# Rounded weight parts from a second transfer on GpSimd's queue, and SSD products in halves of 64 columns, in a hybrid SSD/HGRN2 encoder layer

## The chip, the cores and the metric

The kernel runs on one core of a Trainium2 chip. The metric is the device time of one execution in microseconds (us); the time of a kernel is the median of several executions. TensorE is called PE in the profile (PEld is its loading of stationary operands), VectorE DVE, ScalarE ACT, GpSimd POOL, SyncE SP. A transfer is issued by an engine's queue (SP's or POOL's here) and carried out by 16 DMA engines that all queues share.

## The reference

One encoder layer on 512 tokens of width 1024. Everything is float32.

```
mod = silu(c) @ ada_w + ada_b           # shift1, scale1, gate1, shift2, scale2, gate2
h = rmsnorm(x) * (1 + scale1) + shift1
proj = h @ w_in                         # z, xbc, dt, q, f_fwd, f_bwd, i, g
y_ssd = ssd_mixer(z, xbc, dt, ...)      # 16 heads x 64, state 128, both directions
y_hg  = hgrn2_mixer(q, f_fwd, f_bwd, i, g, ...)   # 8 heads, 128 x 128, both directions
x = x + gate1 * (concat(y_ssd, y_hg) @ w_out)
h = rmsnorm(x) * (1 + scale2) + shift2
x = x + gate2 * (relu(h @ w_up)**2 @ w_down)      # d_ff = 4096
return rmsnorm(x)
# inside the SSD scan, per chunk and head:
w = scores * decay * dt
y_intra = einsum("btsgh,bsghp->btghp", w, xc)
```

## The kernel before

**Two-part products.** To reach float32 accuracy with TensorE's fp32r type, each operand of a weight product is held as two fp32r parts: `hi`, the value rounded to fp32r, and `lo`, the remainder. A product is three matmuls, hi x hi, hi x lo and lo x hi, accumulated in PSUM. The products inside the recurrences are plain float32 matmuls.

**Weights.** Weights come in units: 256 output columns by 1024 rows, in four quarters of 256 rows, each quarter a tile of 128 partitions x 2 x 256 (256 KB). `unit_load` issues the transfers of a unit's quarters from SP into tiles `raw` (four buffers). `unit_split` calls `split` for the quarters asked for: it takes a tile `hi` and a tile `lo` (seven buffers each), lets ScalarE copy `raw` to `hi`, which rounds, and VectorE compute `lo = raw - hi`. `wl_load` does the same for the last column quarter of w_out into tiles `wohi` and `wolo` (eight buffers).

**Units ahead.** While the products of one unit run, the next is loaded, and its quarters 1 to 3 are split at the unit's start; the fourth is split by `last()`, from a hook in the unit's last pass. So the fourth quarter of the next unit gets the buffer of the current unit's first quarter, the seventh before it.

**Stages**, in us of the profiled span: startup with norms and modulation (0 to 68; its own copies of weights, 16 quarters in `su_split`, are not touched by the change); the units of w_in other than z, mixed with the steps of the SSD and HGRN2 recurrences (68 to 459); the four z units (459 to 522); w_out's first 512 columns in 16 iterations, three ahead (522 to 571); its third column quarter in four groups of 4 x 128 rows (574 to 597); its last column quarter from `wohi`, `wolo` (597 to 625); the MLP as four blocks of four up units and four dn units (625 to 989). In the background, rows of `ada_w` are loaded (`adaw`, 512 KB each, from POOL's queue) and summed by VectorE into the later modulation rows (`ada`).

**Order.** TensorE keeps the order in which the code is written. `Clock` adds up estimated costs of what was emitted for TensorE, VectorE and ScalarE; `tick()`, called between products, advances the recurrences' step generators when the clock says they are due and the two vector engines are less than 3.5 us ahead of TensorE. The order on the other engines is set by the framework's scheduler when the program is built. A queue runs in order: an instruction or transfer that waits holds all that stand behind it on its engine.

**SSD.** For each group of heads and each of four blocks of 128 tokens, `load` fetches the cumulated decays of four heads (tile `e`, and `bc` for the other direction, read from the scratch tensor `cdr`) over POOL's queue; `decay` turns them into `es`, 128 x 4 x 128; `intra` multiplies them with `xs`, 64 columns a head, into `ps_y`. `V`, `K`, `Q`, `S`, `kt`, `at`, `hy` and `T` are tiles of the HGRN2 steps.

**Product loops.** `mm_T` has the weights as the stationary side (w_in's transposed units, up), `mm_N` as the moving side; both take a unit's quarters in order, three matmuls for each 128 rows.

Of the kernel before, what the change touches and what calls it, by code (L numbers as in the profile page):

```python
# [9 lines left out]
F32 = mybir.dt.float32  # L10
F32R = mybir.dt.float32r
# [3 lines left out]
MULT, ADD, SUB, MIN, MAX = ALU.mult, ALU.add, ALU.subtract, ALU.min, ALU.max  # L15
PSUM = bass.MemoryType.PSUM

P = 128
# [35 lines left out]
class Clock:  # L54
# [3 lines left out]
    def __init__(self):  # L58
        self.pe = self.dve = self.act = 0.0
        self.done = {}  # L60
        self.end = 0.0
        self.table = None
# [89 lines left out]
def encoder_layer(  # L152
# [7 lines left out]
    nc = tc.nc  # L160
    clock = Clock()
    V, A, G = Timed(nc.vector, clock, "dve"), Timed(nc.scalar, clock, "act"), nc.gpsimd
# [17 lines left out]
    w_out2 = w_out.rearrange("o k n -> (o k) n")  # L180
# [6 lines left out]
    wp = ctx.enter_context(tc.tile_pool(name="wp", bufs=7))  # L187
# [10 lines left out]
    def nm(s):  # L198
        cnt[0] += 1
        return f"{s}_{cnt[0]}"  # L200

    def psum(tag):
        bufs = {"mm": 2, "sc": 3, "tr": 2, "y": 1}[tag]
        return ps.tile([P, 512], F32, tag=tag, name=nm("ps_" + tag), bufs=bufs)

    def tmp():
        return tp.tile([P, 520], F32, tag="t", name=nm("t"))
# [106 lines left out]
    h_hi = actp.tile([P, KD, T], F32R, tag="A_hi", name="h_hi")  # L314
    h_lo = actp.tile([P, KD, T], F32R, tag="A_lo", name="h_lo")

    def load_w(src, k0, nk, col0, ncols):
        raw = wp.tile([P, 544], F32, tag="raw", name=nm("raw"), bufs=4)
        v = raw[:, :nk * ncols].rearrange("p (k n) -> p k n", n=ncols)
        nc.sync.dma_start(out=v, in_=src[k0 * P:(k0 + nk) * P, col0:col0 + ncols].rearrange("(k p) n -> p k n", p=P))  # L320
        return v


    amod = const([P, 16], "amod")
# [275 lines left out]
        yield  # L600


    def split(raw, nk, ncols, lo_eng=None):
        n = nk * ncols
        hi = wp.tile([P, 544], F32R, tag="hi", name=nm("hi"))[:, :n].rearrange("p (k n) -> p k n", n=ncols)
        lo = wp.tile([P, 544], F32R, tag="lo", name=nm("lo"))[:, :n].rearrange("p (k n) -> p k n", n=ncols)
        A.copy(out=hi, in_=raw)
        (lo_eng or V).tensor_tensor(out=lo, in0=raw, in1=hi.bitcast(F32), op=SUB)
        return hi, lo

    def unit_load(src, cols, k0=0):

        ncols = sum(n for _, n in cols)
        quarters = []
        for q in range(4):
            raw = wp.tile([P, 544], F32, tag="raw", name=nm("raw"), bufs=4)
            v = raw[:, :2 * ncols].rearrange("p (k n) -> p k n", n=ncols)
            o = 0
            for c0_, n in cols:
                r = (k0 + 2 * q) * P  # L620
                nc.sync.dma_start(out=v[:, :, o:o + n], in_=src[r:r + 2 * P, c0_:c0_ + n].rearrange("(k p) n -> p k n", p=P))
                o += n
            quarters.append(v)
        return quarters, ncols

    def unit_split(u, qs=range(4)):
        quarters, ncols = u
        return [split(quarters[q], 2, ncols) for q in qs]

    def mm_T(w, j, rh, rl, nk=8, pst=None, n0=0, n=T, hook=None, ks=None):  # L630

# [98 lines left out]
    def ssd_group(g, after):  # L730
# [35 lines left out]
        es, ld = {}, {}  # L766
# [9 lines left out]
        def decay(cc, q):  # L776

            e, bc = ld[cc, q, 0], ld[cc, q, 1]
            h0 = g * 8 + 4 * q
            for d, dst in ((0, e), (1, bc)):  # L780
                if d < DEC:
                    V.tensor_tensor(out=dst, in0=dst, in1=b3(off[:, d, cc, h0:h0 + 4], 4, P), op=ADD)
                else:
                    for h in range(4):
                        A.activation(dst[:, h, :], dst[:, h, :], AF.Identity, bias=off[:, d, cc, h0 + h:h0 + h + 1])
            V.copy_predicated(out=e, mask=masks[:, NL64 * 64:].unsqueeze(1).broadcast_to([P, 4, P]), data=bc)
            A.activation(e, e, AF.Exp)
            V.tensor_tensor(out=e, in0=e, in1=cb[:, g, cc, :].unsqueeze(1).broadcast_to([P, 4, P]), op=MULT)
            es[cc, q] = e
            if q == 0:  # L790
                load(cc, 1, 0)
                load(cc, 1, 1)
            elif cc + 1 < NT:
                load(cc + 1, 0, 1)
# [4 lines left out]
        for cc in range(NT):  # L799
            yv = xs[:, cc, g * 512:(g + 1) * 512]  # L800

            def intra(q):
                for h in range(4):
                    c0_ = (4 * q + h) * 64
                    PE.matmul(out=py[:, c0_:c0_ + 64], lhsT=es[cc, q][:, h, :], rhs=yv[:, c0_:c0_ + 64], start=True, stop=True)

            decay(cc, 0)
            yield -9.0
            decay(cc, 1)
            yield  # L810
            py = psum("y")
            intra(0)
            intra(1)
            dirs = [d for d in range(2) if (d, cc) in st]
            pis = {}
            for d in dirs:
                pis[d] = psum("sc")
                PE.matmul(out=pis[d], lhsT=ct[:, g, cc * P:(cc + 1) * P], rhs=st[d, cc], start=True, stop=True)
            V.tensor_tensor(out=h3(yv), in0=h3(yv), in1=b3(coef[:, cc, hs], 8, 64), op=MULT)
            V.tensor_tensor(out=yv, in0=yv, in1=py, op=ADD)  # L820
            for d in dirs:
                ti = tmp()[:, :512]
                V.tensor_tensor(out=h3(ti), in0=h3(pis[d]), in1=b3(epre[:, d, cc, hs], 8, 64), op=MULT)
                V.tensor_tensor(out=yv, in0=yv, in1=ti, op=ADD)
            yield
            if cc + 1 < NT:
                load(cc + 1, 0, 0)
            yield
# [293 lines left out]
    cols = {"z": O_Z, "x": O_X, "q": O_Q, "ff": O_FF, "fb": O_FB, "i": O_I, "g": O_G}  # L1122
# [69 lines left out]
    korder = list(range(8, 14)) + list(range(8)) + [14, 15]  # L1192

    def mh(k, tt):
        return m_hi[k // 8][:, k % 8, tt * P:(tt + 1) * P]

    def ml(k, tt):
        return m_lo[k // 8][:, k % 8, tt * P:(tt + 1) * P]
# [5 lines left out]


    accs = [psum(t) for t in ("mm", "mm", "y", "sc")]
    wt = [split(load_w(w_out2, korder[i], 1, 0, 512), 1, 512) for i in range(3)]
    late = Stream(clock)
    late.add(mixl, xs, slack=1.0)
    x1 = None  # L1210
    for i in range(16):
        if i + 3 < 16:
            wt.append(split(load_w(w_out2, korder[i + 3], 1, 0, 512), 1, 512))
        hi, lo = wt[i]
        k = korder[i]
        for tt in range(NT):
            mm3(accs[tt], mh(k, tt), ml(k, tt), hi[:, 0, :], lo[:, 0, :], i == 0, i == 15)
            ada_on[0] = i < 12 or not ada_idle[0]
            tick()
        if late.due():  # L1220
            late.advance()
        if i == 12:
            late.drain()
            x1 = ypool.tile([P, NT, D], F32, tag="xs", name="x1")
            for tt in range(NT):
                nc.gpsimd.dma_start(out=x1[:, tt, :], in_=x2d[tt * P:(tt + 1) * P, :])
# [20 lines left out]
    wl_ = []  # L1247

    def wl_load(i):
        raw = load_w(w_out2, korder[i], 2, 768, 256)  # L1250
        hi = wo.tile([P, 2, 256], F32R, tag="hi", name=nm("wohi"))
        lo = wo.tile([P, 2, 256], F32R, tag="lo", name=nm("wolo"))
        A.copy(out=hi, in_=raw)
        V.tensor_tensor(out=lo, in0=raw, in1=hi.bitcast(F32), op=SUB)
        wl_.append((hi, lo))

    for i in range(0, 16, 4):
        ks = korder[i:i + 4]
        wq = [split(load_w(w_out2, ks[2 * q], 2, 512, 256), 2, 256) for q in range(2)]
        for tt in range(2):  # L1260
            for kk in range(4):
                k = ks[kk]
                mm3(accs1[tt][:, :256], mh(k, tt), ml(k, tt), wq[kk // 2][0][:, kk % 2, :], wq[kk // 2][1][:, kk % 2, :], i + kk == 0, i + kk == 15)
            tick()
        if i == 0:
            for tt in range(NT):
                gated_add(accs[tt], tt, 1, slice(0, 512), gate)
            accs1 += [psum("mm"), psum("mm")]
        wl_load(i)
        wl_load(i + 2)  # L1270
        for tt in range(2, NT):
            for kk in range(4):
                k = ks[kk]
                mm3(accs1[tt][:, :256], mh(k, tt), ml(k, tt), wq[kk // 2][0][:, kk % 2, :], wq[kk // 2][1][:, kk % 2, :], i + kk == 0, i + kk == 15)
            tick()
# [42 lines left out]
    for tt in range(NT):  # L1318
        o = psum(("sc", "y", "mm", "mm")[tt])
        for i in range(16):  # L1320
            k = korder[i]
            hi, lo = wl_[i // 2]
# [53 lines left out]
    for i, u in enumerate(units):  # L1376
# [13 lines left out]
        else:  # L1390
# [8 lines left out]
            if u == units[-1]:  # L1399
# [6 lines left out]
                for tt in range(NT):  # L1406
                    o = psum("mm")
# [3 lines left out]
                    r = rs2[:, tt:tt + 1]  # L1411
                    n = 448 if tt == 3 else 768
# [19 lines left out]
            for pair in range(2 if u[2] else 0):  # L1432
                o = psum("mm")
# [40 lines left out]
```

## Time and profile before

| | |
|---|---|
| median of 3 executions | 996.17 us (996.04 to 996.61) |
| the profiled execution | 997.37 us, its span 995.6 us |
| granted TensorE clock, mean | 0.992 |
| DMA traffic | 116.7 MB; SP's queue 86.45 MB, POOL's 28.32 MB |
| POOL's transfers | 32 `e`, 32 `adaw`, some few others |

The span is the time from the first to the last recorded instruction; the execution's time is 1.8 us longer. The profile names an instruction by line, engine, operation and `output<-inputs`, with buffer numbers left out; most rows have the line of a helper that records every instruction (L106 for vector operations, L170 for matmuls). A group's row has its busy time, the mean length of one in ns, and after the second bar the time for which the engine stood idle just before such instructions, with what ended most of that.

### The profile page before, as it was taken

The page shows a single profiled execution, that of the slowest core. Times are in us where ns is not written, and L with a number is a line of the kernel's source. Part 1 is how long each engine was busy: PE and PEld are TensorE (multiplying, and loading weights), DVE is VectorE, ACT ScalarE, POOL GpSimd, SP SyncE. Part 2 cuts the span into 40 slices and gives each one's busy share as a digit, 9 for nine tenths or more (in the row PEclk, how much of TensorE's full clock was granted, in tenths as well). Part 3 has the DMA queues.
Part 4 walks back from the last instruction along what each step waited for, and adds up shares of the span by engine and source line. Part 5 has one row for each costly group of instructions (what it writes and reads, how often), then busy time and mean ns, then how long its engine had stood idle before and what let it go on. Part 6 is the DMA issues. An engine that isn't in the chain of part 4 may idle for free.

```text
span 995.6 us, 17588 instructions
## 1 busy us (share of the span) xinstructions
PE 962.5 (97%) x6886; PEld 843.9 (85%) x6886; DVE 649.2 (65%) x1189; ACT 493.9 (50%) x965; POOL 48.1 (5%) x91
## 2 busy tenths in 40 slices
PE   5999999999999999989999999999999999999997
PEld 4788887788877888879998899979988998998897
DVE  4478869887989475877777677665544455444445
ACT  6367647857675366565555225642233234214414
POOL 0000000010000000000111211000000000000000
PEclk9999999999999989999999999999999999999999
DMA  9953422334422333222656875133332233223322
GB/s 272 266 134 82 111 76 64 86 96 127 109 81 77 97 106 84 66 75 65 191 168 191 283 244 147 58 114 100 98 114 85 86 105 106 88 85 96 105 66 85
DMA packets 114791, 116.70 MB, mean 117 GB/s; under 512 B 8556, under 2 KB 103445, under 8 KB 114709
## 3 DMA queue, kind: packets, MB, share of 16 engines
q1 hardware_dynamic: 106213, 86.45, 29.7%
q0 software_dynamic: 8064, 28.32, 9.2%
q8 instruction: 54, 0.88, 0.4%
q10 hardware_dynamic: 432, 0.82, 0.2%
q14 instruction: 28, 0.23, 0.1%
HBM read 113.39 MB, written 2.16 MB: 116 GB/s over the span
## 4 chain that ended last, share of the span: by engine, by line
PE 87%; DVE 4%; DMA 3%; ACT 3%; issue 2%; SPq 0%; DVEq 0%; ACTq 0%; POOLq 0%
PE ps_mm L170 65%; PE ps_sc L170 13%; PE ps_tr L170 4%; PE ps_y L170 3%; PE ps_tr L175 2%; DMA raw<-in_w_in_dram 1%; DMA e<-cdr 1%; DVE K L106 1%; ACT hi L106 1%; DMA adaw<-in_ada_w_dram 1%; ACT t L106 1%; DVE lo L106 0%; DVE ada L106 0%; DVE Q L106 0%; DVE t L106 0%
## 5 line engine op out<-in xcount | busy, mean ns | idle before, releaser
L106 ACT CAST hi<-raw 128x512 fp32r<-128x512 f32 (+1 forms) x276 | 167.1, 614 | 240.7 <-PE ps_mm L170 156.7
L106 DVE TENSOR_TENSOR lo<-raw,hi 128x512 fp32r<-128x512 f32 (+1 forms) x276 | 185.5, 681 | 108.4 <-ACT hi L106 106.2
L170 PE MATMUL ps_mm<-hi,uh 128*128 128x256 f32 x448 | 125.8, 281 | 0.0
L170 PE MATMUL ps_mm<-hi,ul 128*128 128x256 f32 x448 | 125.4, 280 | 0.0
L170 PE MATMUL ps_mm<-lo,uh 128*128 128x256 f32 x448 | 125.4, 280 | 0.0
L170 PE MATMUL ps_mm<-hi,h_hi 128*128 128x256 f32 (+1 forms) x384 | 114.3, 298 | 0.0
L170 PE MATMUL ps_mm<-h_hi,hi 128*128 128x512 f32 x256 | 107.9, 422 | 1.1 <-ACT h_hi L106 1.1
L170 PE MATMUL ps_mm<-lo,h_hi 128*128 128x256 f32 (+1 forms) x384 | 108.2, 282 | 0.0
L170 PE MATMUL ps_mm<-hi,h_lo 128*128 128x256 f32 (+1 forms) x384 | 108.1, 282 | 0.0
L170 PE MATMUL ps_mm<-h_hi,lo 128*128 128x512 f32 x256 | 101.7, 397 | 0.0
L170 PE MATMUL ps_mm<-h_lo,hi 128*128 128x512 f32 x256 | 101.5, 397 | 0.0
L170 PE MATMUL ps_mm<-m_hi,hi 128*128 128x512 f32 (+1 forms) x264 | 100.7, 381 | 0.7 <-ACT m_hi L106 0.7
L170 PE MATMUL ps_mm<-m_lo,hi 128*128 128x512 f32 (+1 forms) x264 | 100.7, 382 | 0.6 <-DVE m_lo L106 0.6
L170 PE MATMUL ps_mm<-m_hi,lo 128*128 128x512 f32 (+1 forms) x264 | 100.7, 382 | 0.0
L170 PEld LDWEIGHTS ps_mm<-hi,uh 128*128 128x128 f32 x448 | 84.3, 188 | 0.4 <-issue 0.2
L170 PEld LDWEIGHTS ps_mm<-lo,uh 128*128 128x128 f32 x448 | 84.2, 188 | 0.4 <-issue 0.2
L170 PEld LDWEIGHTS ps_mm<-hi,ul 128*128 128x128 f32 x448 | 84.4, 188 | 0.0
L106 ACT ACTIVATE t<-ps_mm 128x512 f32<-128x512 f32 x63 | 37.4, 594 | 76.8 <-PE ps_mm L170 76.2
L170 PEld LDWEIGHTS ps_mm<-hi,h_hi 128*128 128x128 f32 x384 | 72.4, 189 | 3.5 <-issue 1.7
L170 PEld LDWEIGHTS ps_mm<-lo,h_hi 128*128 128x128 f32 x384 | 72.5, 189 | 1.9 <-issue 1.7
L170 PEld LDWEIGHTS ps_mm<-hi,h_lo 128*128 128x128 f32 x384 | 72.4, 189 | 0.0
L106 DVE TENSOR_TENSOR t<-t 128x512 f32<-128x512 f32 x32 | 22.1, 692 | 64.9 <-ACT uh L106 64.9
(301 smaller groups left out, 1967.6 us busy)
## 6 DMA issues: line engine op xcount, KB each, us to landing
raw<-in_w_in_dram SPq DMA_DIRECT2D x68, 256.0 KB, 2.9
adaw<-in_ada_w_dram POOLq DMA_DIRECT2D x32, 512.0 KB, 5.1
raw<-in_w_up_dram SPq DMA_DIRECT2D x64, 256.0 KB, 3.0
raw<-in_w_down_dram SPq DMA_DIRECT2D x64, 256.0 KB, 3.1
raw<-in_w_in_dram SPq DMA_DIRECT2D x104, 128.0 KB, 2.8
ada_in<-in_ada_w_dram SPq DMA_DIRECT2D x16, 512.0 KB, 6.1
e<-cdr POOLq DMA_DIRECT2D x32, 256.0 KB, 3.6
raw<-in_w_out_dram SPq DMA_DIRECT2D x32, 256.0 KB, 5.1
```

Of the source, the lines that this page charges most:

```text
L106: return f(*args, **kw)
L170: return tc.keep_in_program_order(nc.tensor.matmul(**kw))
L175: return tc.keep_in_program_order(nc.tensor.transpose(**kw))
```

## The change

`load_w`, `split` and the loading half of `unit_load` become a class `Weights`. It loads `raw` from SP as before. Its `split` no longer copies: it issues a second transfer of the same weights from HBM, from POOL's queue, into the fp32r tile `hi`, and this transfer rounds. VectorE's `lo = raw - hi` stays. `hi` no longer depends on `raw`, and a `raw` buffer is free again when `lo` is computed. Quarters that are put together from two column ranges (`h0`, `h1`, `h2`, and the first unit, with its 16 columns for dt) take two transfers for `hi`, as they do for `raw`. Since there is no `A.copy`, the clock does not count one.

Second, each of the 64 float32 matmuls in `intra` (128 stationary columns of `es`, 64 moving columns) is split in two with 64 stationary columns each, into the lower and the upper half of PSUM's partitions.

```diff
-    def load_w(src, k0, nk, col0, ncols):
-        raw = wp.tile([P, 544], F32, tag="raw", name=nm("raw"), bufs=4)
-        ...
+    class Weights:
+        def __init__(self, src, k0, nk, cols):
+            self.nk, self.ncols, self.parts = nk, sum(n for _, n in cols), []
+            raw = wp.tile([P, 544], F32, tag="raw", name=nm("raw"), bufs=4)
+            self.raw = self.view(raw)
+            o = 0
+            for c0_, n in cols:
+                self.parts.append((o, n, src[k0 * P:(k0 + nk) * P, c0_:c0_ + n].rearrange("(k p) n -> p k n", p=P)))
+                o += n
+            for o, n, ap in self.parts:
+                nc.sync.dma_start(out=self.raw[:, :, o:o + n], in_=ap)
+        ...
+        def split(self, hi=None, lo=None):
+            hi = self.view(wp.tile([P, 544], F32R, tag="hi", name=nm("hi"))) if hi is None else hi
+            for o, n, ap in self.parts:
+                nc.gpsimd.dma_start(out=hi[:, :, o:o + n], in_=ap)
+            lo = self.view(wp.tile([P, 544], F32R, tag="lo", name=nm("lo"))) if lo is None else lo
+            V.tensor_tensor(out=lo, in0=self.raw, in1=hi.bitcast(F32), op=SUB)
+            return hi, lo
 ...
-    def split(raw, nk, ncols, lo_eng=None):
-        ...
-        A.copy(out=hi, in_=raw)
-        (lo_eng or V).tensor_tensor(out=lo, in0=raw, in1=hi.bitcast(F32), op=SUB)
-        return hi, lo
 ...
     def unit_split(u, qs=range(4)):
-        quarters, ncols = u
-        return [split(quarters[q], 2, ncols) for q in qs]
+        return [u[q].split() for q in qs]
 ...
-                    PE.matmul(out=py[:, c0_:c0_ + 64], lhsT=es[cc, q][:, h, :], rhs=yv[:, c0_:c0_ + 64], start=True, stop=True)
+                    for t0 in (0, 64):
+                        PE.matmul(out=py[t0:t0 + 64, c0_:c0_ + 64], lhsT=es[cc, q][:, h, t0:t0 + 64], rhs=yv[:, c0_:c0_ + 64],
+                                  start=True, stop=True)
 ...
     def wl_load(i):
-        raw = load_w(w_out2, korder[i], 2, 768, 256)
         hi = wo.tile([P, 2, 256], F32R, tag="hi", name=nm("wohi"))
         lo = wo.tile([P, 2, 256], F32R, tag="lo", name=nm("wolo"))
-        A.copy(out=hi, in_=raw)
-        V.tensor_tensor(out=lo, in0=raw, in1=hi.bitcast(F32), op=SUB)
-        wl_.append((hi, lo))
+        wl_.append(Weights(w_out2, korder[i], 2, [(768, 256)]).split(hi, lo))
```

w_out's first half and its third quarter use `Weights(...).split()` in the same way.

ScalarE in the mixed stage, at 362 us of the profiled execution, where the evicted `V` of an HGRN2 head stands between decays (`e`), copies (`hi`) and the other steps. Before:

```order
L106 COPY hy_4020<-K_647_3665 128x512
L106 ACTIVATE e_3841<-e_3841,off 128x128
L106 CAST hi_3920<-raw_3747 128x512
L106 ACTIVATE e_3841<-e_3841,off 128x128
L106 CAST hi_3985<-raw_3973 128x512
L106 ACTIVATE e_3841<-e_3841,off 128x128
L106 CAST hi_3989<-raw_3976 128x512
L106 COPY V_3762<-ps_mm_3843 128x512
L106 CAST hi_3993<-raw_3979 128x512
L106 ACTIVATE e_3841<-e_3841,off 128x128
```

The same eviction now:

```order
L106 COPY hy_4075<-K_647_3737 128x512
L106 ACTIVATE e_3879<-e_3879,off 128x128 x4
L106 COPY hy_4202<-K_647_3737 128x512
L106 COPY V_3845<-ps_mm_3937 128x512
L106 COPY S_4058<-ps_tr_4050 128x384
```

The four copies of weights are gone; the four steps of the decay and one more copy of an HGRN2 step stand ahead of the eviction.

POOL at the end of the z units (`adaw` are the background's rows; `hi<-in_w_in` are quarters of z units, `hi<-in_w_out` w_out's first). Before, POOL's queue has the background alone; its ninth and tenth `adaw` are the last two here:

```order
L436 DMA adaw_5449<-in_ada_w_dram 128x2x512
L436 DMA adaw_5451<-in_ada_w_dram 128x2x512
L436 DMA adaw_5502<-in_ada_w_dram 128x2x512
L436 DMA adaw_5506<-in_ada_w_dram 128x2x512
L436 DMA adaw_5615<-in_ada_w_dram 128x2x512
L436 DMA adaw_5617<-in_ada_w_dram 128x2x512
```

Now:

```order
L337 DMA hi_5492<-in_w_in_dram 128x2x256
L455 DMA adaw_5605<-in_ada_w_dram 128x2x512
L455 DMA adaw_5609<-in_ada_w_dram 128x2x512
L455 DMA adaw_5731<-in_ada_w_dram 128x2x512
L455 DMA adaw_5733<-in_ada_w_dram 128x2x512
L337 DMA hi_5652<-in_w_in_dram 128x2x256
L337 DMA hi_5814<-in_w_out_dram 128x512
```

The seventh to the tenth `adaw` now stand between the third and the fourth quarter (`hi_5652`) of the last z unit.

More of the change, by code (lines that the diff above doesn't have):

```diff
@@ L315, in encoder_layer, with view @@
     h_lo = actp.tile([P, KD, T], F32R, tag="A_lo", name="h_lo")
-    def load_w(src, k0, nk, col0, ncols):
-        raw = wp.tile([P, 544], F32, tag="raw", name=nm("raw"), bufs=4)
-        v = raw[:, :nk * ncols].rearrange("p (k n) -> p k n", n=ncols)
-        nc.sync.dma_start(out=v, in_=src[k0 * P:(k0 + nk) * P, col0:col0 + ncols].rearrange("(k p) n -> p k n", p=P))
-        return v
+    class Weights:
[9 more added lines that the diff above has]
+                nc.sync.dma_start(out=self.raw[:, :, o:o + n], in_=ap)
+        def view(self, t):
+            return t[:, :self.nk * self.ncols].rearrange("p (k n) -> p k n", n=self.ncols)
+        def split(self, hi=None, lo=None):
[5 more added lines that the diff above has]
+            return hi, lo
     amod = const([P, 16], "amod")
@@ L600, in scores_ssd @@
         yield
-    def split(raw, nk, ncols, lo_eng=None):
-        n = nk * ncols
-        hi = wp.tile([P, 544], F32R, tag="hi", name=nm("hi"))[:, :n].rearrange("p (k n) -> p k n", n=ncols)
-        lo = wp.tile([P, 544], F32R, tag="lo", name=nm("lo"))[:, :n].rearrange("p (k n) -> p k n", n=ncols)
-        A.copy(out=hi, in_=raw)
-        (lo_eng or V).tensor_tensor(out=lo, in0=raw, in1=hi.bitcast(F32), op=SUB)
-        return hi, lo
-    def unit_load(src, cols, k0=0):
[L613 to L624, printed above, removed]
+    def unit_load(src, cols, k0=0):
+        return [Weights(src, k0 + 2 * q, 2, cols) for q in range(4)]
     def unit_split(u, qs=range(4)):
-        quarters, ncols = u
-        return [split(quarters[q], 2, ncols) for q in qs]
+        return [u[q].split() for q in qs]
     def mm_T(w, j, rh, rl, nk=8, pst=None, n0=0, n=T, hook=None, ks=None):
@@ L1206, in encoder_layer @@
     accs = [psum(t) for t in ("mm", "mm", "y", "sc")]
-    wt = [split(load_w(w_out2, korder[i], 1, 0, 512), 1, 512) for i in range(3)]
+    wt = [Weights(w_out2, korder[i], 1, [(0, 512)]).split() for i in range(3)]
     late = Stream(clock)
@@ L1212, in encoder_layer @@
         if i + 3 < 16:
-            wt.append(split(load_w(w_out2, korder[i + 3], 1, 0, 512), 1, 512))
+            wt.append(Weights(w_out2, korder[i + 3], 1, [(0, 512)]).split())
         hi, lo = wt[i]
@@ L1249, in wl_load @@
     def wl_load(i):
-        raw = load_w(w_out2, korder[i], 2, 768, 256)
         hi = wo.tile([P, 2, 256], F32R, tag="hi", name=nm("wohi"))
         lo = wo.tile([P, 2, 256], F32R, tag="lo", name=nm("wolo"))
-        A.copy(out=hi, in_=raw)
-        V.tensor_tensor(out=lo, in0=raw, in1=hi.bitcast(F32), op=SUB)
-        wl_.append((hi, lo))
+        wl_.append(Weights(w_out2, korder[i], 2, [(768, 256)]).split(hi, lo))
     for i in range(0, 16, 4):
         ks = korder[i:i + 4]
-        wq = [split(load_w(w_out2, ks[2 * q], 2, 512, 256), 2, 256) for q in range(2)]
+        wq = [Weights(w_out2, ks[2 * q], 2, [(512, 256)]).split() for q in range(2)]
         for tt in range(2):
```

## The prediction

> **What bounds the kernel now.** I read the page first (busy shares, chain, groups, DMA issues), then what TensorE waits for, then the places where a new wait could stand. Busy time, the chain of waits by engine, and the two costliest groups:
>
> ```profile
> PE 962.5 (97%) x6886; PEld 843.9 (85%) x6886; DVE 649.2 (65%) x1189; ACT 493.9 (50%) x965; POOL 48.1 (5%) x91
> PE 87%; DVE 4%; DMA 3%; ACT 3%; issue 2%; SPq 0%; DVEq 0%; ACTq 0%; POOLq 0%
> L106 ACT CAST hi<-raw 128x512 fp32r<-128x512 f32 (+1 forms) x276 | 167.1, 614 | 240.7 <-PE ps_mm L170 156.7
> L106 DVE TENSOR_TENSOR lo<-raw,hi 128x512 fp32r<-128x512 f32 (+1 forms) x276 | 185.5, 681 | 108.4 <-ACT hi L106 106.2
> ```
>
> TensorE is busy 97% of 995.6 us. ScalarE's copies are 167 us of work, but of an engine that is half idle: 16 of the 276 stay (startup), so 260 x 0.614 = 160 us leave ScalarE, and this is worth no more than the TensorE waits that those copies cause. All of TensorE's waits from 70 to 523 us, the stage in which weight products and the two recurrences are mixed, that exceed 1 us (us in total, times, longest):
>
> ```profile
> PE ps_sc L170 <- DVE S L106: 3.6, 2, 2.3
> PE ps_tr L170 <- ACT V L106: 2.2, 1, 2.2
> PE ps_tr L170 <- ACT S L106: 2.0, 3, 0.8
> PE ps_tr L175 <- ACT bn L106: 1.1, 1, 1.1
> ```
>
> Together 8.9 us, of which ScalarE's is 5.3. So the gain has a low ceiling, and a loss has none: the question is whether `hi` from the DMA arrives as early as ScalarE delivered it.
>
> **Gain 1: ScalarE's copies out of the way.** ScalarE (start, duration) and then TensorE around the largest wait, with another gap of TensorE below it; and the clock in the stretch after it (us; busy of PE, PEld, DVE, ACT, POOL; granted clock; DMA share; GB/s):
>
> ```profile
> 361.71 0.40 ACT L106 ACTIVATE e<-e,off 128x128 f32<-128x128 f32 x1 [1.41 <-DMA e<-cdr]
> 362.02 0.60 ACT L106 CAST hi<-raw 128x512 fp32r<-128x512 f32 x1
> ...
> 363.64 0.60 ACT L106 CAST hi<-raw 128x512 fp32r<-128x512 f32 x1
> 364.15 0.57 ACT L106 COPY V<-ps_mm 128x512 f32<-128x512 f32 x1
> ```
> ```profile
> 361.95 0.61 PE L170 MATMUL ps_tr<-V,kt 128*128 128x128 f32 x4
> ...
> 283.71 0.46 PE L170 MATMUL ps_sc<-S,Q 128*128 128x128 f32 x2 [1.25 <-DVE S L106]
> ```
> ```profile
> 365.00:372.00 7.00, 7.00 (x27) 5.60 (x27) 4.22 (x11) 1.92 (x5) 1.08 (x2) 0.52 0.64 192
> ```
>
> TensorE stands until V is copied, and V stands behind three copies of `hi` between the rows shown (one takes 364.15 - 363.64 = 0.51 of the queue, three 1.5). After the gap the granted clock is 0.52 for 7 us, which costs 7.0 x 0.48 = 3.4 us. Without the copies V comes 1.5 us earlier and the gap shrinks from 2.2 to 0.7; the gap of 1.25 us at 283 us had no such aftermath, so I take the 3.4 as gone too: -4.9. The other ScalarE waits are short; a third of S goes, -0.6. Against that, the planner no longer books ScalarE for the copies, so the steps of the recurrences and with them the order of VectorE's queue move everywhere in this stage; the two waits for VectorE's S (3.6) can vanish or get company, which I put at 0 (-4 to +8; the upper end is one more gap of 2.3 with its clock, 5.7, and another of 2.3). Sum of gain 1: -5.5 (-10 to +4).
>
> Is `hi` late here? Its buffers are seven deep; counting products from the last reader of a buffer to the first reader of its next content in the new order, at the durations of their rows, gives 7.5 to 28 us in this stage, against a landing of some 4 us (below). And POOL's queue: the `hi` transfers now stand in one row with the decays `e<-cdr`, each waiting for its own buffer. A transfer that waits holds the others, but the `e` loads lead their use by 8 us or more and most `hi` have twice that, so I put 0 on it, with up to 3 in the range.
>
> **Gain 2: SSD products in halves.** TensorE's rows of one set (the last but one) and, ahead of it, of products of another part whose stationary side has 64 columns and whose moving side has the same 64:
>
> ```profile
> 408.85 0.69 PE L170 MATMUL ps_sc<-q,hy 128*64 128x64 f32 x16
> 409.36 0.84 PE L170 MATMUL ps_sc<-Q,hy 128*64 128x64 f32 x16
> 410.13 0.39 PE L170 MATMUL ps_mm<-hi,h_hi 128*128 128x256 f32 x1
> ...
> 413.91 1.89 PE L170 MATMUL ps_y<-xs,e 128*128 128x64 f32 x16
> 415.64 1.08 PE L170 MATMUL ps_sc<-st,ct 128*128 128x512 f32 x2
> ```
>
> A set takes 415.64 - 413.91 = 1.73 us. The 64-column rows take 0.51 and 0.77 per 16, and the new set has 32: 1.02 to 1.54 us. It saves 0.2 to 0.7, eight times: -1.6 to -5.6. I take -3.4, near the middle.
>
> **Loss 1: the fourth quarter between dn units.** The last transfer of a unit gets the buffer of the current unit's first quarter, which is read until 18 products before that unit's end; it is first needed 18 products after it. One such place; ScalarE, VectorE and TensorE:
>
> ```profile
> 785.11 2.73 ACT L106 CAST hi<-raw 128x512 fp32r<-128x512 f32 x4 [8.52 <-PE ps_mm L170]
> 785.76 2.10 DVE L106 TENSOR_TENSOR lo<-raw,hi 128x512 fp32r<-128x512 f32 x3 [2.75 <-ACT hi L106]
> ```
> ```profile
> 785.02 0.28 PE L170 MATMUL ps_mm<-lo,uh 128*128 128x256 f32 x1
> ...
> 787.13 0.28 PE L170 MATMUL ps_mm<-lo,uh 128*128 128x256 f32 x1
> ```
>
> From 785.02 to 787.13 are 18 products, 0.117 each, so `hi` has 36 x 0.117 = 4.2 us less 0.1 for the release, and `lo` 0.1 more. Before, copy and difference took 0.6 + 0.7 of them. Now a whole transfer lies in them. For what POOL's transfers take, the group rows (KB each, median us from issue to landing), then the smallest, median and largest for `e`:
>
> ```profile
> raw<-in_w_down_dram SPq DMA_DIRECT2D x64, 256.0 KB, 3.1
> e<-cdr POOLq DMA_DIRECT2D x32, 256.0 KB, 3.6
> adaw<-in_ada_w_dram POOLq DMA_DIRECT2D x32, 512.0 KB, 5.1
> raw<-in_w_out_dram SPq DMA_DIRECT2D x32, 256.0 KB, 5.1
> ```
> ```profile
> DMA to landing us min/median/max: 3.3/3.6/4.8
> ```
>
> `e` has the size and the queue of `hi`; `hi` has rows of 1 KB and a rounding, which no row shows, so 3.3 to 5.1, and I take 3.8. Then `lo` is ready 0.1 + 3.8 + 0.1 + 0.7 = 4.7 after the release, needed after 4.2: a stall of 0.5. By the same sum 3.3 gives 0.2 and 5.1 gives 1.8. Such neighbours are dn1-dn2 and dn2-dn3 of four blocks, 8 in all: +4 (+1.6 to +14). Up units and dn0-dn1 have 6 to 8 us and stay hidden. The rule on the other side is in the Trainium skill's "DMA: Bandwidth & Descriptors", section "Anatomy of one DMA": its fit of 2.0 us and the bytes at 436 GB/s would give, as an estimate, 2.6 us for 256 KB and no stall at all here. The 256 KB row of the same queue, 3.6, is a microsecond longer, and the row decides.
>
> The z units have the same product pattern in their N-form and the last of them has 4.1 us; there the transfer also stands behind four `adaw` transfers on POOL, the last of which waits for VectorE's sums. The row of that one before:
>
> ```profile
> 510.14 0.72 POOL L436 DMA_DIRECT2D adaw<-in_ada_w_dram  x1 [1.64 <-DVE ada L106]
> ```
>
> Counted on the products, the buffer is free at 507.6 and needed at 511.7; if the `adaw` of 510.14 goes first, landing is at 510.9 + 3.8 and `lo` at 515.4, 3.7 late. The background runs a little earlier when ScalarE is freer; I take +2 (0 to 6).
>
> **Loss 2: the start of the MLP.** Of the second up unit, the fourth quarter's buffer is read until 18 products (2.1 us) before the product at 641.77 that needs it:
>
> ```profile
> 640.29 2.18 ACT L106 CAST hi<-raw 128x512 fp32r<-128x512 f32 x4
> 641.77 0.28 PE L170 MATMUL ps_sc<-m_hi,hi 128*128 128x256 f32 x1
> ```
>
> 2.1 us are left for 4.7, where copy and difference now take 1.3 for the first of four: +2.6 (1 to 4).
>
> **Loss 3: w_out.** The DMA engines there, same columns as above:
>
> ```profile
> 571.00:580.00 9.00, 9.00 (x68) 8.51 (x68) 8.40 (x15) 1.18 (x2) 0.63 (x2) 1.00 0.57 203
> 580.00:590.00 10.00, 10.00 (x86) 10.00 (x86) 6.60 (x11) 3.36 (x6) 2.04 (x3) 1.00 0.81 274
> 590.00:597.00 7.00, 7.00 (x62) 7.00 (x61) 4.24 (x7) 2.78 (x5) 0.72 (x1) 1.00 0.90 280
> 597.00:610.00 13.00, 13.00 (x114) 13.00 (x113) 9.56 (x27) 8.06 (x17) 0.67 (x1) 1.00 0.50 156
> ```
>
> Full engines move 274/0.81 = 338 GB/s. From 571 to 597 another 16 x 256 KB = 4.2 MB are asked for, 12.4 us of full engines, and free are 9 x 0.43 + 10 x 0.19 + 7 x 0.10 = 6.5. The rest, 6 us, spills into 597 to 610, where as much is free and the later half of these parts is used. Earlier loading takes some of it (seven `hi` buffers do not wait for `raw`), and what ScalarE took between `raw` and `lo` is saved: +2.5 (0 to 8). The Trainium skill, same page, section "Latency and other measured facts", gives 0.2 us for an access to memory on average and 2 us at high load; by that a landing here would be, as an estimate, 3.6 + 1.8 = 5.4 us. The trace agrees in kind: the same 256 KB from SP land in 3.1 us in the MLP and in 5.1 for w_out.
>
> **Sum.** -5.5 - 3.4 + 4 + 2 + 2.6 + 2.5 = +2.2. The profiled execution took 997.37 us (995.6 span, 1.8 around it), 1.2 over the median of the runs, 996.17. So 999.6 for such an execution, 998.4 against the median. What a measurement of this kernel tells from no change is about 0.2%, 2 us; the sum is just over that.
>
> **Rivals.** *Transfers hidden, faster (0.35).* If a rounding transfer lands within 3.0 us of the release, the eight dn neighbours and z cost nothing (-6 against my sum); the point is 4.2 - 0.9 = 3.3 us. For it: `raw` of the same bytes and rows lands in 3.1 from SP. Against: the fastest of 32 `e` took 3.3. The fit cited under loss 1 is this rival's page. With w_out hidden by earlier loading, 998.4 - 6 - 2.5 = 990; with part of that, 990 to 994.
>
> *Rounding transfers are slow (0.2).* Landing at 5.1, as `raw` for w_out shows under load: dn +14 instead of +4, z +5, start of MLP +4, w_out +6: 998.4 + 18 = about 1016; half of it, 1007. For it: DMA bytes rise from 117 to 185 MB, and the transfers now come in pairs with `raw`. Against: MLP's DMA share is 0.2 to 0.3 now and stays near half.
>
> *A new gap with the clock behind it (0.1).* One VectorE wait of over 2 us in the mixed stage and 7 us at half clock: +5.7, gain 1 becomes a loss, 1004 to 1008.
>
> *The copies never mattered (within the first case).* If the gap at 362 stays for another reason (V waits for the decays too), 4.9 comes back: 1003.
>
> **How the numbers follow.** My case (0.35): 998.4, 995 to 1003. Of it a tenth is faster by over 0.2%, four tenths within 0.2% (994.2 to 998.2), half slower: 0.03, 0.14, 0.18. The first rival gives 0.32 faster and 0.03 within; the second and third 0.30 slower. Sums 0.35, 0.17, 0.48. The range holds 8 in 10 with 988 to 1010: below lie deeper gains (0.06), above the heavy half of the slow case (0.12).
>
> **What would show it.** Each step: ScalarE busy 494 less 160 = 334; POOL's rows up by some 320 transfers, and their median landing near 3.8; no gap at V and no clock of 0.52 around 360; ps_y sets of 1.0 to 1.5 us; in the MLP, eight short TensorE waits (0.2 to 1.8) for `lo` or the DMA at the dn neighbours, one of 2 to 3 at the first unit; w_out's DMA share at 0.9 or more with TensorE waiting for `hi` or `lo`. I am wrong if the landing is outside 3.3 to 5.1, if VectorE's new order makes or removes waits of several microseconds in the mixed stage, or if w_out's transfers starve.

## The result and the profile after

The changed kernel takes 1036.66 us (median of 4), the kernel before 996.11 on the same chip: ratio 1.041 (1.0383 to 1.0437). That is 40 us slower, where 998.4 with a range of 988 to 1010 was forecast. Rows of the page of the changed kernel: the busy shares, the costliest group of VectorE and that of POOL, and one row of the DMA issues (KB each, median us from issue to landing):

```profile
PE 978.0 (94%) x7014; PEld 850.4 (82%) x7014; DVE 651.0 (63%) x1189; ACT 343.2 (33%) x699; POOL 276.1 (27%) x411
L106 DVE TENSOR_TENSOR lo<-raw,hi 128x512 fp32r<-128x512 f32 (+1 forms) x276 | 186.2, 682 | 181.6 <-DMA hi<-in_w_up_dram 43.9
L337 POOL DMA_DIRECT2D hi<-in_w_in_dram x160 | 114.9, 726 | 221.7 <-PE ps_mm L170 200.2
hi<-in_w_down_dram POOLq DMA_DIRECT2D x64, 256.0 KB, 3.7
```

ScalarE lost 151 us of work (160 forecast), and a rounding transfer lands in 3.7 us, as forecast (3.8). But VectorE now stands 181.6 us in front of its `lo` (108.4 before), though one `lo` takes no longer than it did (682 ns against 681). TensorE is idle for 1036.2 - 978.0 = 58 us of the span instead of 33. The mean granted clock fell from 0.992 to 0.973; by an estimate this is worth about another 20 us (0.027 x 1036 against 0.008 x 996), most of which are counted as busy.

By stages (mixed, z, w_out, MLP; us from and to; busy of PE, PEld, DVE, ACT, POOL; granted clock; DMA share; GB/s), before and then after:

```profile
68.00:459.00 391.00, 381.26 (x2927) 320.51 (x2926) 308.98 (x566) 252.80 (x501) 18.98 (x35) 0.99 0.32 86
459.00:522.00 63.00, 62.38 (x567) 60.12 (x566) 46.02 (x82) 35.67 (x91) 8.54 (x12) 1.00 0.53 162
522.00:625.00 103.00, 100.17 (x664) 90.55 (x663) 72.01 (x135) 43.09 (x83) 15.47 (x23) 1.00 0.67 215
625.00:977.00 352.00, 351.15 (x2297) 319.43 (x2298) 177.46 (x291) 120.22 (x207) 1.42 (x2) 1.00 0.29 91
```
```profile
66.00:476.00 410.00, 389.41 (x3085) 323.69 (x3084) 310.31 (x571) 206.50 (x414) 120.75 (x176) 0.96 0.63 144
476.00:539.00 63.00, 60.17 (x535) 57.71 (x535) 44.37 (x77) 23.90 (x70) 17.48 (x26) 1.00 0.75 206
539.00:661.00 122.00, 108.97 (x666) 97.75 (x664) 72.81 (x136) 23.76 (x50) 38.02 (x57) 0.93 0.86 259
661.00:1018.00 357.00, 353.68 (x2300) 320.42 (x2301) 178.94 (x290) 48.91 (x86) 88.13 (x123) 1.00 0.66 178
```

Mixed +19, w_out +19, MLP +5, z nothing; the startup was 2 us shorter in this execution. In the mixed stage TensorE's waits are these (total, times, longest), for results of VectorE above all:

```profile
PE ps_sc L170 <- DVE S L106: 7.2, 2, 3.6
PE ps_y L170 <- DVE e L106: 6.4, 2, 4.3
PE ps_tr L170 <- DVE sa L106: 3.7, 1, 3.7
PE ps_tr L170 <- ACT kt L106: 2.1, 1, 2.1
```

And this is what one of them looks like on VectorE (start, duration), and TensorE's row that waits for the last line:

```profile
249.26 0.44 DVE L106 COPY_PREDICATED at<-masks,ps_sc 128x256 f32<-128x256 uint8 x1
252.66 0.69 DVE L106 TENSOR_TENSOR lo<-raw,hi 128x512 fp32r<-128x512 f32 x1 [2.96 <-DMA hi<-in_w_in_dram]
253.27 0.76 DVE L106 COPY_PREDICATED e<-masks,e 128x512 f32<-128x512 uint8 x1
253.90 0.69 DVE L106 TENSOR_TENSOR lo<-raw,hi 128x512 fp32r<-128x512 f32 x1
254.50 0.76 DVE L106 SCALAR_TENSOR_TENSOR Q<-q,lbs,T 128x512 f32<-128x512 f32 x1
255.16 0.70 DVE L106 TENSOR_TENSOR lo<-raw,hi 128x512 fp32r<-128x512 f32 x1
255.76 0.69 DVE L106 TENSOR_TENSOR e<-e,cb 128x512 f32<-128x512 f32 x1
```
```profile
256.51 0.72 PE L170 MATMUL ps_y<-xs,e 128*64 128x64 f32 x14 [2.10 <-DVE e L106]
```

TensorE does not need this `lo` soon: it is the first quarter of the next unit, whose products start at 268.48, 15 us after the row's end. But it stands in VectorE's queue, `hi` has not landed, and the decay behind it waits 2.96 us; TensorE then stands 2.1 us for the decay.

### The profile page after: what moved, and what is told of

Same layout as the page of the kernel before. It is cut to its first block, busy times and chain, and to the rows that moved or that the text cites. A ratio compares the mean times of both kernels' runs of the same rounds, so it can differ in the third digit from the quotient of the medians.

```text
span 1036.2 us, 17999 instructions
## 1 busy us (share of the span) xinstructions
PE 978.0 (94%) x7014; PEld 850.4 (82%) x7014; DVE 651.0 (63%) x1189; ACT 343.2 (33%) x699; POOL 276.1 (27%) x411
## 4 chain that ended last, share of the span: by engine, by line
issue 24%; PE 23%; DMA 7%; POOL 6%; DVE 3%; ACT 0%; POOLq 0%; DVEq 0%; ACTq 0%
PE ps_mm L170 20%; POOL hi L337 5%; PE ps_sc L170 2%; DMA hi<-in_w_out_dram 2%; DMA adaw<-in_ada_w_dram 2%; DMA hi<-in_w_up_dram 1%; DMA hi<-in_w_in_dram 1%; DVE ada L106 1%; POOL adaw L455 1%; DMA hi<-in_w_down_dram 1%; DMA raw<-in_w_out_dram 1%; DVE lo L106 0%; DMA e<-cdr 0%; DVE t L106 0%; PE ps_tr L170 0%
## 5 line engine op out<-in xcount | busy, mean ns | idle before, releaser
L106 DVE TENSOR_TENSOR lo<-raw,hi 128x512 fp32r<-128x512 f32 (+1 forms) x276 | 186.2, 682 | 181.6 <-DMA hi<-in_w_up_dram 43.9
L337 POOL DMA_DIRECT2D hi<-in_w_in_dram x160 | 114.9, 726 | 221.7 <-PE ps_mm L170 200.2
L170 PE MATMUL ps_mm<-h_hi,hi 128*128 128x512 f32 x256 | 110.8, 433 | 1.1 <-ACT h_hi L106 1.1
L337 POOL DMA_DIRECT2D hi<-in_w_down_dram x64 | 45.9, 720 | 136.8 <-PE ps_mm L170 100.9
L337 POOL DMA_DIRECT2D hi<-in_w_up_dram x64 | 45.9, 721 | 133.8 <-PE ps_mm L170 132.1
```

Of the source, the lines that this page charges most:

```text
L106: return f(*args, **kw)
L170: return tc.keep_in_program_order(nc.tensor.matmul(**kw))
L337: nc.gpsimd.dma_start(out=hi[:, :, o:o + n], in_=ap)
```

## The experiments

TensorE's instructions stand in the same order in e1_halves and e3_booked, and in the order of the changed kernel in all others but e10_unbooked_only, e11_gap_short and e12_gap_long. Times are medians; ratios are to the kernel before on the same chip. The stage times in the text are from first product to first product in the traces, that is, of one profiled execution each.

**Planner or transfers: a table of two by two.** All with halves: the copies on ScalarE or the transfer, the copy counted by the planner's clock or not. The fourth cell is the changed kernel.

e1_halves:

```diff
 # the kernel before, and in intra():
+for t0 in (0, 64):
+    PE.matmul(out=py[t0:t0 + 64, c0_:c0_ + 64], lhsT=es[cc, q][:, h, t0:t0 + 64], rhs=yv[:, c0_:c0_ + 64], ...)
```

> The kernel before with the halves of 64 alone; copies stay on ScalarE. Both theories (transfers on POOL's queue as the cause, or the planner's new order as the cause) expect the sets of products to shrink from 1.73 us to 1.0 to 1.5 and the time to be 990 to 995; a time above 998 would put part of the loss on the halves themselves, through the small shift in the planner's costs.

e2_unbooked, on e1_halves:

```diff
-A.copy(out=hi, in_=raw)            # A: counted by the clock
+nc.scalar.copy(out=hi, in_=raw)
```

> Halves, hi by ScalarE's copies from raw, but the clock does not count them: TensorE's order is word for word that of the changed kernel, and there is no second transfer. If the planner's new order costs what the mixed stage lost (+19 us from 68 to 459), this takes 1008 to 1015. If the transfers cost it, 990 to 997.

e3_booked, on the changed kernel:

```diff
 nc.gpsimd.dma_start(out=hi[:, :, o:o + n], in_=ap)
+clock.op("act", (), dict(out=hi, in_=self.raw))
```

> The changed kernel, but the clock counts a copy on ScalarE for every split though none is made: TensorE's order is word for word that of e1_halves, hi comes by the second transfer. If the planner's order is to blame for the mixed stage, only w_out (+19) and the MLP (+4) stay: 1013 to 1020. If the transfers are, 1030 to 1040.

| with halves | copies on ScalarE | transfer |
|---|---|---|
| copy counted | e1_halves 987.78, 0.9936 (0.9911 to 0.996) | e3_booked 1035.2, 1.0421 (1.0394 to 1.0448) |
| copy not counted | e2_unbooked 979.5, 0.9862 (0.9844 to 0.988) | the change 1036.66, 1.041 (1.0383 to 1.0437) |

The transfers cost 47 to 48 us in the one order and 55 to 57 in the other (by the medians and the ratios). The planner's new order is no loss: with the copies it gains 8 us. So e1_halves came out 2 us and e2_unbooked 10 us under what had been expected. In e2_unbooked the mixed stage takes 377.4 us, 390.8 before, 409.6 after the change, and hardly a wait of TensorE is left there (its longest three):

```profile
PE ps_tr L170 <- ACT kt L106: 0.8, 1, 0.8
PE ps_tr L175 <- ACT st L106: 0.6, 1, 0.6
PE ps_y L170 <- DVE e L106: 0.5, 1, 0.5
```

So the change held a gain that the transfers hid, and e2_unbooked is faster than both kernels. The halves do what they were to do; TensorE's row of the last set in the changed kernel, and the next row:

```profile
424.83 1.15 PE L170 MATMUL ps_y<-xs,e 128*64 128x64 f32 x32
425.92 1.12 PE L170 MATMUL ps_sc<-st,ct 128*128 128x512 f32 x2
```

1.09 us instead of 1.73, for eight sets 5.1 us, where no wait falls into a set.

**The new order alone.** e10_unbooked_only, the edit of e2_unbooked on the kernel before.

> The kernel before with the copies not counted by the clock, nothing else: no halves, no transfers. e2_unbooked against e1_halves gave -8; if the two effects add, this is 8 us under before (-0.8%); if the order pays only together with the halves, within 2 us of before.

984.68, ratio 0.9901 (0.9886 to 0.9917): -1.0%. The halves' -0.6% and this add up to e2_unbooked's -1.4% within the intervals.

**Who waits for the transfer.** e5_lo_own, on the changed kernel:

```diff
-V.tensor_tensor(out=lo, in0=self.raw, in1=hi.bitcast(F32), op=SUB)
+nc.scalar.copy(out=lo, in_=self.raw)
+V.tensor_tensor(out=lo, in0=self.raw, in1=lo.bitcast(F32), op=SUB)
```

> The changed kernel (hi by transfer, same order of TensorE, same queue of POOL), but lo no longer waits for the transfer: ScalarE copies raw into the lo tile and VectorE subtracts in place. Only TensorE still waits for hi. If the loss is VectorE's queue, stopped at lo until the transfer lands, with all steps of the recurrences behind it, most comes back: 980 to 990. If the loss is POOL's queue (e and adaw held behind waiting hi transfers) or the traffic, VectorE's freedom changes little: 1020 to 1035.

1000.84, ratio 1.0039 (1.002 to 1.0059): 36 of the 57 us come back, though the transfers and TensorE's order are as they were and POOL's queue nearly so. The expectation's 980 to 990 was too hopeful by 11 us. The mixed stage goes from 409.6 to 384.0; e2_unbooked has 377.4. Most of the rest is lost in w_out (115.5 against 103.0). VectorE's longest waits from 66 to 516 us, the changed kernel and then e5_lo_own:

```profile
DVE lo L106 <- DMA hi<-in_w_in_dram: 31.5, 25, 3.0
DVE lo L106 <- issue: 15.3, 16, 3.3
DVE e L106 <- ACT e L106: 10.1, 7, 4.2
```
```profile
DVE e L106 <- ACT e L106: 17.3, 10, 3.9
DVE lo L106 <- ACT lo L339: 15.3, 22, 4.0
DVE Q L106 <- PE ps_sc L170: 12.2, 14, 3.1
```

In these rows 47 us of standing before `lo` become 15, as much as in e2_unbooked (15.4); "issue" is a wait for which the profile shows no releaser. Two more things move with this edit. ScalarE copies weights again, and the framework's scheduler orders VectorE's queue anew: with `lo` left aside, some 110 of VectorE's 905 instructions stand elsewhere than in the changed kernel, and some 40 elsewhere than in e2_unbooked. So the run shows that this part of the loss hangs on `lo` reading the transfer. How much of it is the wait as such, and how much the order that the scheduler made for a `lo` of this kind, it does not separate.

In the MLP, from the third up unit to the last dn unit, what was lost (+2.4 us against e2_unbooked) shrinks to 0.4: between dn units TensorE itself gets `hi` in time, or nearly so.

**The decays behind the transfers.** e6_e_sp: the changed kernel with `load` issuing `e` from `nc.sync` instead of `nc.gpsimd`.

> The changed kernel with the decays e loaded from SP's queue instead of POOL's. If hi transfers that wait for their buffers hold the e loads behind them, the mixed stage gets 10 to 30 us back: 1007 to 1027. If VectorE's waits for the landing are the cause, nothing changes beyond 3 us: 1033 to 1040.

1032.82, ratio 1.0371 (1.0321 to 1.0421), not to be told from the changed kernel's 1.041. The mixed stage took 405.0 instead of 409.6 in the traces. `e` lands no sooner there (median 4.3 us in both, 3.6 before); on SP's queue it stands among the `raw` transfers instead. At most a small part lies in the place of `e` behind `hi`.

**Traffic that nobody waits for.** e7_traffic, on the changed kernel:

```diff
-nc.gpsimd.dma_start(out=hi[:, :, o:o + n], in_=ap)
+nc.gpsimd.dma_start(out=dummy[:, :, o:o + n], in_=ap)      # scratch in HBM
+nc.scalar.copy(out=hi, in_=self.raw)
```

> hi by ScalarE's copies (not counted by the clock, order of TensorE as in the changed kernel), and beside it the same second rounding transfer of every quarter from POOL's queue, but into a scratch tensor in HBM that nobody reads: the traffic and POOL's issues without the dependence. If the load on the DMA engines or on POOL's queue is the cause, 1010 to 1035; if it is that somebody waits for the transfers, as e2_unbooked, 979 to 986.

1069.1, ratio 1.0727 (1.0703 to 1.0751). This one missed its aim: with no buffer to wait for, the scratch transfers ran ahead and kept the DMA engines full for the first third of the span, the startup included (40 us lost by the first product of the mixed stage). It says nothing on the spread traffic of the change, so e9_paced ties each scratch transfer to its copy:

```diff
-nc.gpsimd.dma_start(out=hi[:, :, o:o + n], in_=ap)
+nc.scalar.copy(out=hi, in_=self.raw)
+nc.gpsimd.dma_start(out=dummy[:, :, o:o + n], in_=hi[:, :, o:o + n])
```

> Copies as in e2_unbooked, and of every hi quarter, once copied, a transfer of the same size from POOL's queue into a scratch tensor in HBM that nobody reads; unlike in e7_traffic each waits for its copy, so the traffic is spread as in the changed kernel and e and adaw stand among these transfers. If traffic or POOL's queue is enough to cost the mixed stage its 35 us, 1005 to 1035; if somebody must wait for the transfers, 980 to 995, with most of the difference to e2_unbooked in w_out.

995.6, ratio 1.0004 (0.9985 to 1.0024): 16 us above e2_unbooked by the medians, 14 by the ratios, just outside what was expected for "somebody must wait". The profiled execution was the slowest of ten (999.13, the fastest 993.03); in it 14.4 us more lie in the mixed stage (391.8 against 377.4), most of them in two gaps of 2.95 and 2.68 us with their clock, and 5 in w_out. These transfers go from the chip's on-chip memory to HBM, those of the changed kernel the other way. So 70 MB more through POOL's queue are not free even when nobody waits for their data: in this kernel the decays and `adaw` stand between them. Whether it is the queue or the slower landing (`raw` for w_in 4.5 us here, 3.2 in e2_unbooked) was not separated.

**w_out.** e4_wout_copy: the changed kernel, with `A.copy(out=hi, in_=self.raw)` for w_out's 32 quarters.

> The changed kernel with w_out's 32 quarters copied by ScalarE again; all other hi by transfer. Theory of the queue: w_out lost 19 us because adaw's waits on POOL hold the hi transfers, so about 1018 to 1022. If the loss there is the DMA engines' load or VectorE's order instead, with the background sums in the way, less comes back: 1025 to 1035.

1021.88, ratio 1.0292 (1.0263 to 1.032): w_out takes 104.7 us instead of 122.5. That the transfers there do it is shown; that `adaw`'s waits hold them is not, because e5_lo_own, with nearly the same queue, takes 115.5. The DMA issues of e5_lo_own in that stage (KB each, median us to landing), and under them those of e2_unbooked:

```profile
adaw<-in_ada_w_dram POOLq DMA_DIRECT2D x18, 512.0 KB, 7.2
raw<-in_w_out_dram SPq DMA_DIRECT2D x25, 256.0 KB, 7.1
hi<-in_w_out_dram POOLq DMA_DIRECT2D x19, 256.0 KB, 6.7
```
```profile
adaw<-in_ada_w_dram POOLq DMA_DIRECT2D x18, 512.0 KB, 5.4
raw<-in_w_out_dram SPq DMA_DIRECT2D x25, 256.0 KB, 4.9
```

e8_half_adaw, on e5_lo_own, takes load away and leaves the queue:

```diff
-nc.gpsimd.dma_start(out=avs[i], in_=ada2[2 * i * P:2 * (i + 1) * P, ...])
+nc.gpsimd.dma_start(out=avs[i][:, 0, :], in_=ada2[2 * i * P:(2 * i + 1) * P, ...])
-ada_acc(acc, avs[k // 2][:, k % 2, :], k)
+ada_acc(acc, avs[k // 2][:, 0, :], k)
```

> e5_lo_own (lo free of the transfer), and each background load of ada_w brings only its first 128 rows, which the sums use twice: half of the rows of ada_w are left out of the modulation, the number of transfers, waits and sums stays, 256 KB instead of 512 KB each. e5_lo_own still lost 13 us against e2_unbooked from 516 to 633 us, with the DMA share at 1.16 at 560 to 600. If that is the load on the DMA engines, 6 to 12 us come back: 988 to 995. If it is hi waiting behind adaw's waits in POOL's queue, at most 3: 997 to 1003.

992.56, ratio 0.9971 (0.9955 to 0.9987), against 1.0039 of e5_lo_own: w_out 108.5 instead of 115.5, `raw` lands in 4.9 instead of 7.1. So of w_out's 19 us about 7 went with VectorE's wait for the landing, about 7 with load taken off the DMA engines; the last 5 are open.

**What a gap costs.** After each long gap of the changed kernel the granted clock is low. Whether the gap does that was tried in the MLP of e2_unbooked, four times, in dn unit 1 of each block:

```diff
+g_ = tmp()[:, :T]
+nc.vector.tensor_copy(out=g_, in_=o)
+for _ in range(1):                 # e12_gap_long: 6
+    nc.vector.tensor_tensor(out=g_, in0=g_, in1=g_, op=MAX)
+PE.transpose(out=pg[:, :P], in_=g_[:, :P], identity=ident)
```

> e2_unbooked with four added waits of TensorE, in the second dn unit of each MLP block: VectorE copies the finished product and runs one more operation on the copy, and a transpose on TensorE reads it. A wait of about 1.5 us each (0.2 + 2 x 0.6, and the transpose). The changed kernel's trace has no drop of the granted clock after its gap of 1.5 us: so +6 to 8 in all, 986 to 988. If each gap costs a stretch at half clock whatever its length, +20.

> The same with six operations after the copy: four waits of about 4.5 us. If a wait of this length brings half clock behind it, as after the gaps of 3.5 us in the changed kernel (0.50, then 0.75 over ten us, some 3.4 us lost each): +18 of waits and +13 of clock, 1009 to 1013. If those drops have another cause in the mixed stage, 997 to 999.

990.54, ratio 0.9955 (0.9934 to 0.9976), and 1014.05, ratio 1.018 (1.0148 to 1.0212). The gaps came out at 1.98 and 6.09 us, longer than planned, and both times lie above what was expected (986 to 988, 1009 to 1013). The first gap and what follows, e11_gap_short and then e12_gap_long (the granted clock is the third number from the end):

```profile
672.40:674.50 2.10, 0.12 (x2) 0.05 (x2) 1.99 (x4) 0.00 (x0) 0.00 (x0) 1.00 0.00 0
674.50:682.00 7.50, 7.50 (x59) 7.02 (x60) 3.20 (x6) 2.48 (x4) 0.00 (x0) 1.00 0.14 42
```
```profile
681.40:684.00 2.60, 2.60 (x13) 2.60 (x14) 0.00 (x0) 0.00 (x0) 0.00 (x0) 0.50 0.03 6
684.00:691.00 7.00, 7.00 (x47) 6.52 (x47) 2.55 (x4) 2.39 (x4) 0.00 (x0) 0.83 0.11 36
691.00:701.00 10.00, 10.00 (x88) 10.00 (x87) 4.01 (x8) 1.33 (x3) 0.00 (x0) 1.00 0.26 81
```

In the profiled executions, from the first dn product to the last, the short gaps add 9.2 us (323.6 against 314.4 in e2_unbooked); they last 7.9. The long ones last 24.4 and add 35.4 (349.8): 2.7 us more each, and the granted clock in the 12 us behind each of them (0.79, 0.80, 0.76, 0.74) gives as much. So a gap of 6 us brings the drop.

For the short gaps the answer holds for this one execution. It was the fastest of ten (987.99, mean clock 0.997, as in every run of e2_unbooked); most of the others show a mean clock of 0.992 to 0.996 and took up to 995.11. Whether the clock fell behind these gaps there, no trace shows.

## Why the prediction was wrong, step by step

**The step that failed** is "Is `hi` late here?" in gain 1. It counted from buffer to product, that is, for TensorE, found 7.5 us or more, and priced the landing in the mixed stage at 0. The first to wait for `hi` is VectorE, at a `lo` that its queue holds among the recurrences' steps. With TensorE's order the same, the transfers made the mixed stage 32 us longer (409.6 against 377.4 in e2_unbooked), and 26 of these came back when `lo` no longer read the transfer (384.0 in e5_lo_own). The working did say that VectorE's order moves, but gave it 0 (-4 to +8) as an effect of the planner alone; by itself the planner's order was a gain of 10 us (e10_unbooked_only). The second term that was far too small is loss 3, w_out (below).

**ScalarE's copies and the clock behind a gap.** Forecast -5.5, because the copies leave ScalarE's queue. No run shows this mechanism. In e10_unbooked_only the mixed stage is 8.5 us shorter (382.3 against 390.8), TensorE's longest wait for `V` is 0.2 us and the granted clock is 1.00, but all copies are still on ScalarE: it is the planner's order, put at 0, that took the gap away, so the nearness of 5.5 and 8.5 is luck. Where TensorE's order stayed and the copies went, from e1_halves to e3_booked, the wait for `V` grew from 1.5 to 4.4 us. ScalarE and TensorE there:

```profile
371.43 1.28 ACT L106 ACTIVATE e<-e,off 128x128 f32<-128x128 f32 x4 [1.65 <-DMA e<-cdr]
372.62 0.60 ACT L106 COPY hy<-K 128x512 f32<-128x512 f32 x1
373.12 0.58 ACT L106 COPY V<-ps_mm 128x512 f32<-128x512 f32 x1
```
```profile
373.75 1.65 PE L170 MATMUL ps_tr<-V,kt 128*128 128x128 f32 x6 [4.38 <-ACT V L106]
```

No copy of weights stands ahead of `V`; decays that wait for `e` do. This is what the prediction's last rival ("the copies never mattered") named as its condition, though here the transfers may be why `e` is late. In the changed kernel the wait for `V` was 0.8 us, but the transfers brought more gaps than the copies had. The forecast knew the price of a gap, 2.3 and 3.4 us, and allowed one more with its clock; the changed kernel has eight of 2.5 to 4.3 us, four in the mixed stage and four in w_out, each with a lowered clock behind it.

**Halves**: forecast -3.4 (-1.6 to -5.6), measured -5.1 by the rows. The time of e1_halves is lower by 5.6 us by the medians and 6.4 by the ratio (0.64%, interval 0.4 to 0.9%); part of that is not the halves, since TensorE's wait for `V` is 1.5 us there instead of 2.2. The rows lie in the range, towards its far end.

**Between dn units**: forecast +4 for eight neighbours. One of them after the change, VectorE, POOL and TensorE:

```profile
827.53 0.69 DVE L106 TENSOR_TENSOR lo<-raw,hi 128x512 fp32r<-128x512 f32 x1 [0.95 <-DMA hi<-in_w_down_dram]
```
```profile
824.05 2.87 POOL L337 DMA_DIRECT2D hi<-in_w_down_dram  x4 [8.43 <-PE ps_mm L170]
```
```profile
828.28 0.38 PE L170 MATMUL ps_mm<-lo,uh 128*128 128x256 f32 x1 [0.20 <-DVE lo L106]
```

From issue to the start of `lo` 3.5 us, and TensorE stands 0.2. From the third up unit to the last dn unit together 2.4 us (328.9 against 326.5 in the stage times). The fit in the Trainium skill's "DMA: Bandwidth & Descriptors", section "Anatomy of one DMA", gives 2.6 us as an estimate, by which nothing would have been left to wait for; the group's row has 3.7, and the row decides.

**z**: forecast +2; the z stage took 63.3 instead of 62.7 (60.7 in e2_unbooked, so +2.6 with TensorE's order the same). **Start of the MLP**: forecast +2.6; the first two up units took 27.7 against 25.7, +2.0.

**w_out**: forecast +2.5 (0 to 8), measured +19 (122.5 against 103.4). The sum of free DMA time was of the right kind, and e8_half_adaw shows the load to be real, but it let the transfers spill into a stretch with room. It left out that `raw` too lands later under that load (6.2 us, median in this stage), that `lo` then holds VectorE, with `ada` and the additions to x behind it, and that each of the four TensorE gaps there has its clock behind it (0.93 over 122 us is 8.5 us). VectorE's longest waits in that stage of the changed kernel:

```profile
DVE ada L106 <- DMA adaw<-in_ada_w_dram: 12.9, 6, 4.3
DVE lo L106 <- DMA raw<-in_w_out_dram: 11.4, 6, 3.0
DVE lo L106 <- DMA hi<-in_w_out_dram: 9.6, 6, 4.2
```

Here `lo` stands for `raw` at least as long as for `hi`, so a `lo` that is free of `hi` gets only a part back.

**The rivals.** None had this size. The slow case expected landings of 5.1 us and priced the dn units with them; outside w_out the landing stayed at 3.6 to 3.7, and the loss of the mixed stage came where no product was near. The gap in the mixed stage was a rival with one gap at 1004 to 1008; it was the right kind, several times over.

## What to carry to other kernels

When a value that an engine made at once is instead fetched by a transfer, ask of every instruction that reads it what stands behind that instruction in its own queue, not only when the last consumer needs the result: 15 us of slack for TensorE were no cover for a VectorE that had to stop 3 us. Free an idle engine only where its queue delays something; here leaving the copies on ScalarE and merely not counting them in the planner gave 1.0% (984.68), and with the halves 1.4% (979.5). And price a TensorE gap at more than its length: in the changed kernel each of 2.5 us and more had a lowered clock behind it, which by an estimate (12 us times what the granted clock there, 0.72 to 0.88, lacks to 1) cost 1.4 to 3.4 us more. Shorter gaps may bring it or not.

## What the runs showed of the hardware

- A rounding transfer of 256 KB from GpSimd's queue lands in 3.6 to 3.7 us (medians), no later than the plain `e` of before (3.6); under w_out's load it took 5.5 in the changed kernel and 6.7 in e5_lo_own.
- In the profiled executions, four TensorE gaps of 1.98 us left the granted clock at 1.00; four of 6.09 us brought 0.50 and cost 2.7 us each beyond their length. Otherwise the length alone does not decide: gaps of 2.22 us (before, at 362) and 1.53 us (e3_booked, at 554; 0.61 from 557 to 560.5) had the drop behind them, and gaps of 2.35 us (before, at 432) and 2.27 us (e3_booked, at 288) had not (1.00). The Trainium skill, "TensorE: Matmul & The Clock Gate", part 1, has the half clock after at least one idle window of about 3.4 us; the drops after 2.22 and 1.53 us came after less than that, and the measurement decides.
- About 70 MB more through GpSimd's queue, read by nobody, cost 14 to 16 us spread out (e9_paced, from on-chip memory to HBM) and about 90 when it ran ahead (e7_traffic, from HBM to HBM).
